# The products of w_ada with c on PE in four column groups, and the recurrent branch's gate projection as four steps

## The chip, the cores and the metric

The kernel runs on one core of a Trainium2 chip. The metric is the device time of one execution in microseconds. PE is the matmul engine (TensorE), PEld its weight loads, DVE the vector engine, ACT the scalar engine, POOL the engine called GpSimd, SP the engine that issues most of the DMAs. One DMA queue of SP carries the weights.

## The reference

All data are float32. There are 256 positions and 1024 channels. A vector c modulates both halves of the block by 6 x 1024 numbers (shift, scale and gate, twice). The part that matters, cut from the reference:

```python
ada = (jax.nn.silu(c) @ w_ada[layer] + b_ada[layer])[:, None, :]
sh1, sc1, g1, sh2, sc2, g2 = jnp.split(ada, 6, axis=-1)
h = rmsnorm(x, norm_pre_mix[layer]) * (1.0 + sc1) + sh1
proj = h @ w_in[layer] + b_in[layer]
xr, gr, q, k, v, gate_r, gate_a = jnp.split(proj, split_points, axis=-1)
xr = causal_depthwise_conv(xr, conv_w[layer], conv_b[layer])
y_rnn = rg_lru(xr, ...) * jax.nn.gelu(gr)
y_att = swa_sink_attention(q.reshape(...), k.reshape(...), v.reshape(...), attn_sinks[layer])
merged = (jax.nn.sigmoid(gate_r) * (y_rnn @ w_o_rnn[layer])
          + jax.nn.sigmoid(gate_a) * (y_att @ w_o_attn[layer]))
mix = merged @ w_out[layer]
x = x + g1 * rmsnorm(mix, norm_post_mix[layer])
h = rmsnorm(x, norm_pre_ffn[layer]) * (1.0 + sc2) + sh2
ff = moe_ffn(h, ...)            # top 4 of 32 experts, each 1024 -> 2 x 1024 -> 1024
x = x + g2 * rmsnorm(ff, norm_post_ffn[layer])
```

w_ada is 1024 x 6144, 24 MiB; xr and gr are 1024 columns of w_in each, 4 MiB each. h can't be formed before sh1 and sc1, that is, before the first third of w_ada has been multiplied with c. The experts' weights are 384 MiB.

## The kernel before

All weights come through a ring of 18 SBUF tiles of 1 MiB (RING), requested by SP in an order written out by hand. The order of work on every engine is that of the code.

**First stage.** x is normalised and transposed (xnT). Then a loop over the 8 blocks k of 128 channels: w_ada's tile for the block holds two outputs' rows (sh1 and sc1 of the block, transposed by the host, so that one output stands in one partition), and `ada_dot` (L130) multiplies each, 128x1024, with silu(c) broadcast over all partitions, and adds up along the row, on DVE. From the two sums come am (L219 and the line behind it) and hT, the block's modulated input (L225). Each weight tile is split (L166, L169) into hi (fp32r, by ACT) and lo = w − hi (half of it by DVE, half by POOL); hT likewise (`split_h`, L184). A product in full precision is then three fp32r products: hi·hTh, hi·hTl, lo·hTh, called terms here. Each k multiplies w_g1, the weights of xr and gr together, 16 groups of 128 outputs, into all 8 PSUM banks (3 with the tag "p", 5 with the tag "a"): 48 products (L235), for k = 0 sixteen in plain f32 (L228).

**Steps.** 26 steps follow, one weight tile of 1 MiB and 256 output channels each, 48 products (`mm_pair`, L259; step 5 `mm_v`, L178): 0 to 4 k and q, 5 v, 6 to 13 the two merge gates, 14 to 17 and 18 to 21 the two output projections, 22 to 25 w_out. A step splits the next step's tile and evacuates the bank of the step before. PLAN says which small tasks stand in the middle of a step's products and which behind them: the recurrence (block-diagonal products L333), the attention (scores L405, transposes L463, values L475) and, as "A", two `ada_dot`s for one of the 16 tiles of w_ada that remain. ISSUE says at which of three points of each step SP requests what: w the next step's weights, a a tile of w_ada, e the first expert's w1.

**Experts.** After w_out (L598 and around) and the router (L714), 32 experts run through the ring (products L963, L996).

Of the kernel before, what the change touches and what calls it, by code (L numbers as in the profile page):

```python
# [32 lines left out]
PLAN = {0: ('', 'g0 s1'), 1: ('', 'h0 c1 s0 c0'), 2: ('A', 'g1 m1 A'), 3: ('R1 A M00 m0', 'h1 A R0 X00'), 4: ('d1 M01', 's3 X01'), 5: ('d0 M02', 'X02 E00 D0 A M10 A'), 6: ('', 'M11 N00 X10 M12'), 7: ('E01 s2 X11 N01', 'X12 T000 A'), 8: ('P00 T010', 'E10 c2 A T011'), 9: ('P01 m2', 'N10 c3 E11'), 10: ('', 'N11 D1 g3 q0 q1 S0 T100'), 11: ('P10 A T110', 'R2 T111 g2 m3'), 12: ('R3 P11', 'h2 A'), 13: ('S1', 'h3 d2 D2 d3 D3 A'), 14: ('', 'q2 S2 q3 y0 S3'), 15: ('A y2', ''), 16: ('y1', 'A'), 17: ('', 'A y3'), 19: ('', 'A A')}  # L33
ISSUE = {-1: 'wwaww', 0: 'aw', 2: 'w', 5: 'a', 8: 'aw', 11: 'w', 14: 'aa', 19: 'aw', 21: 'w', 22: 'aw', 28: 'w', 29: 'w', 31: 'w', 33: 'a', 36: 'aa', 37: 'aw', 42: 'w', 43: 'wawwa', 49: 'w', 50: 'w', 52: 'awa', 54: 'w', 60: 'w', 64: 'e', 69: 'ww', 71: 'e', 72: 'e', 74: 'e', 76: 'eee'}
# [15 lines left out]
def tile_hybrid_block(ctx: ExitStack, tc: tile.TileContext, x_in, c, vecs, rows, w_ada, w_g1, w_qk, w_v, w_gate,  # L50
# [16 lines left out]
    def rtile(shape, name):  # L67
        return ring.tile([P] + list(shape), F32, name=name, tag="w")
# [70 lines left out]
    ada_dot(wada[0], 0, 0)  # L139
# [11 lines left out]
    ada_dot(wada[0], 1, 8)  # L151
# [8 lines left out]
    def split(w, pool=True, mid=lambda: None):  # L160

        hi, lo = [ring.tile([P, 2 * D], F32R, name=n_, tag="w") for n_ in ("hi", "lo")]
        parts = []
        for h in range(2):
            c_ = slice(h * D, (h + 1) * D)
            nc.scalar.activation(hi[:, c_], w[:, c_], AF.Copy)  # L166
            if h == 0:
                mid()
            (nc.gpsimd if h and pool else nc.vector).tensor_tensor(lo[:, c_], w[:, c_], hi[:, c_], op=OP.subtract)  # L169
            parts.append((hi[:, c_], lo[:, c_]))  # L170
        return parts
# [31 lines left out]
    g1b = [bank("p") for _ in range(3)] + [bank("a") for _ in range(5)]  # L203
    PLAIN = 1

    def g1(f):
        return g1b[f // 2][:, (f % 2) * S:(f % 2 + 1) * S]

    for k in range(KC):
        if k:  # L210
            wada.append(rtile((2, D), "w"))
            for n in range(2):
                nc.sync.dma_start(out=wada[k][:, n], in_=w_ada[k, :, n])
            ada_dot(wada[k], 0, k)
            ada_dot(wada[k], 1, 8 + k)
        wt = rtile((2048,), "w")
        for h in range(2):
            nc.sync.dma_start(out=wt[:, h * D:(h + 1) * D], in_=w_g1[k, :, h * D:(h + 1) * D])
        nc.vector.scalar_tensor_tensor(am[:, 0, k:k + 1], ada[:, 8 + k:9 + k], scb[:, k:k + 1], v("n_pre_mix", k),  # L219
                                       op0=OP.add, op1=OP.mult)  # L220
        nc.vector.tensor_tensor(am[:, 1, k:k + 1], ada[:, k:k + 1], vec[:, o_ + k:o_ + k + 1], op=OP.add)
        if k == 1:
            lru_scales()
        hT[k] = t2((S,), name="hT")
        nc.vector.tensor_scalar(hT[k], xnT[:, k], am[:, 0, k:k + 1], am[:, 1, k:k + 1], op0=OP.mult, op1=OP.add)  # L225
        if k < PLAIN:
# [3 lines left out]
        else:  # L230
            whl = split(wt, mid=lambda: split_h(k))
            for h in range(2):
                for i, (m, n) in enumerate(THREE):
                    for f in range(8):
                        nc.tensor.matmul(g1(8 * h + f), whl[h][m][:, f * P:(f + 1) * P], (hTh, hTl)[n][:, k], start=False,  # L235
                                         stop=k == KC - 1 and i == 2, skip_group_check=True)
        if 4 <= k < 4 + PLAIN:
            split_h(k - 4)
# [246 lines left out]
    W = [w_qk[i] for i in range(5)] + [w_v] + [w_gate[i] for i in range(8)]  # L485
# [86 lines left out]

    evac = [ev_k] + [lambda b, i=i: ev_q(i, b) for i in range(4)] + [ev_v]
    evac += [lambda b, i=i: ev_gate(i, b) for i in range(8)]
    evac += [lambda b, i=i: merge_a(i, b) for i in range(4)] + [lambda b, i=i: merge_r(i, b) for i in range(4)]
    for i in range(22):
        if i == 14:
# [3 lines left out]
        if i == 0:  # L581
            for f in range(8):
                b_ = g1b[4 + f // 2][:, (f % 2) * S:(f % 2 + 1) * S]
                nc.vector.tensor_scalar(gr[:, f], b_, v("b_gr", f), None, op0=OP.add)
        run(after)
    nc.vector.tensor_tensor(ada[:, 16:48], ada[:, 16:48], vec[:, o_ + 16:o_ + 48], op=OP.add)
# [750 lines left out]
```

## Time and profile before

| | |
|---|---|
| median of 3 runs | 1278.45 us (1278.22 to 1279.37) |
| the profiled execution | 1279.63 us, its span 1278.0 us |
| busy in the span | PE 1157.3, DVE 525.8, ACT 261.6, POOL 136.9 us |
| first stage (all products of xr and gr) | 14.26 to 72.13 us |
| steps 0 to 21 | 72.13 to about 267 us |
| w_out, router | about 267 to 313 us |
| experts | about 313 us to the end |

Busy times add up the instructions of one engine. The span is the time from the first instruction to the last; the rows further down are stretches, groups and single instructions of the same execution.

### The profile page before, as it was taken

What the parts mean: (1) busy time and instruction counts of PE and PEld (TensorE: products, weight loads), DVE (VectorE), ACT (ScalarE), POOL (GpSimd) and SP (SyncE); (2) the same over time, 40 slices, a digit from 0 to 9 for tenths busy, and PEclk for the clock granted to TensorE, in tenths of its full rate; (3) what the DMA queues carried; (4) which work ended last, traced back from release to release, by engine and by line L of the source; (5) the groups of instructions that cost most, each with busy time, mean ns of one, the idle gap of its engine ahead of it and who ended that gap; (6) DMA issues with size and microseconds to landing.
All of it is one profiled execution on the core that took longest, in us unless ns stands there. A gap on an engine that the chain in (4) does not pass through costs nothing. (4 is left out here: it accounts for less than half of the span.)

```text
span 1278.0 us, 15323 instructions
## 1 busy us (share of the span) xinstructions
PE 1157.3 (91%) x5883; PEld 554.6 (43%) x5883; DVE 525.8 (41%) x914; ACT 261.6 (20%) x482; POOL 136.9 (11%) x79
## 2 busy tenths in 40 slices
PE   7897978879899999999999988988999999999986
PEld 5896768767333333333333222323333333333322
DVE  6999988965332223232223222222033232322222
ACT  4265656324210001100011001100010011100002
POOL 2355555320100000000000000000000000000000
PEclk9998989889989999999999999999999999999998
DMA  9963436667989999999999999999999999999993
GB/s 366 393 240 144 176 119 255 263 262 288 391 329 379 421 421 421 421 422 421 421 420 421 422 422 421 421 421 421 420 421 418 421 422 421 421 420 420 421 420 123
DMA packets 68177, 468.73 MB, mean 367 GB/s; under 512 B 7616, under 2 KB 8000, under 8 KB 13696
## 3 DMA queue, kind: packets, MB, share of 16 engines
q1 hardware_dynamic: 67392, 466.67, 89.1%
q10 hardware_dynamic: 704, 1.01, 0.3%
q8 instruction: 47, 0.77, 0.2%
q14 instruction: 34, 0.28, 0.1%
HBM read 466.61 MB, written 1.05 MB: 366 GB/s over the span
## 5 line engine op out<-in xcount | busy, mean ns | idle before, releaser
L963 PE MATMUL bank_a<-w,xg 128*64 128x512 f32 x2048 | 469.2, 601 | 9.1 <-DMA w<-in_w_dram 8.9
L963 PEld LDWEIGHTS bank_a<-w,xg 128*64 128x64 f32 x2048 | 137.3, 137 | 290.7 <-issue 251.4
L996 PE MATMUL bank_a<-w,aT 128*64 128x512 f32 x960 | 219.6, 602 | 12.9 <-ACT aT L990 7.4
L1044 DVE TENSOR_SCALAR G<-bank_p,slot 128x256 fp32r<-128x256 f32 x32 | 15.5, 484 | 415.6 <-PE bank_p L1039 415.6
L996 PEld LDWEIGHTS bank_a<-w,aT 128*64 128x64 f32 x960 | 65.3, 138 | 150.1 <-issue 108.6
L990 ACT ACTIVATE aT<-bank_p 128x512 f32<-128x512 f32 x31 | 18.5, 597 | 530.6 <-PE bank_p L986 530.6
L1017 DVE TENSOR_TENSOR ff<-ff,bank_p 128x512 f32<-128x512 f32 x124 | 79.6, 683 | 63.5 <-PE bank_p L1014 63.5
L169 POOL TENSOR_TENSOR lo<-w,hi 128x1024 fp32r<-128x1024 f32 x32 | 89.8, 2809 | 132.5 <-ACT hi L166 105.7
L1251 POOL TENSOR_TENSOR os<-os,x 128x512 f32<-128x512 f32 x1 | 1.8, 1821 | 875.4 <-ACT os L1250 875.4
L130 DVE SCALAR_TENSOR_TENSOR w<-w,cs 128x1024 f32<-128x1024 f32 x48 | 89.4, 1900 | 1.1 <-DMA w<-in_w_ada_dram 1.1
L1004 DVE SCALAR_TENSOR_TENSOR ys<-bank_a,gslot,ys 128x512 fp32r<-128x512 f32 x31 | 23.2, 750 | 151.6 <-ACT ys L1003 151.6
L166 ACT ACTIVATE hi<-w 128x1024 fp32r<-128x1024 f32 x66 | 66.1, 1050 | 11.7 <-DVE lo L169 6.8
L1014 PE MATMUL bank_p<-ys,G 64*128 64x512 f32 x248 | 47.3, 457 | 14.1 <-DVE ys L1004 13.5
L1003 ACT ACTIVATE ys<-bank_a,gslot 128x512 fp32r<-128x512 f32 x31 | 21.3, 688 | 172.0 <-PE bank_a L996 168.5
L169 DVE TENSOR_TENSOR lo<-w,hi 128x1024 fp32r<-128x1024 f32 x34 | 49.0, 1445 | 6.9 <-ACT hi L166 6.9
L777 PE MATMUL bank_p<-pm,hth 128*128 128x256 f32 x112 | 33.4, 327 | 13.4 <-DVE pm L759 13.4
L1014 PEld LDWEIGHTS bank_p<-ys,G 64*128 64x128 f32 x248 | 19.3, 191 | 47.0 <-issue 25.2
L777 PEld LDWEIGHTS bank_p<-pm,hth 128*128 128x128 f32 x112 | 22.7, 203 | 35.9 <-issue 18.3
L959 PE MATMUL bank_a<-b1r,pick 128*128 128x512 f32 x124 | 37.7, 423 | 0.0
L976 ACT ACTIVATE ys<-gl 128x512 f32<-128x512 f32 x33 | 20.8, 630 | 69.4 <-DVE gl L975 69.4
L959 PEld LDWEIGHTS bank_a<-b1r,pick 128*128 128x128 f32 x124 | 20.7, 188 | 29.4 <-issue 26.8
L259 PE MATMUL bank_p<-hTh,hi 128*128 128x256 f32 x208 | 31.2, 294 | 0.0
(337 smaller groups left out, 1252.2 us busy)
## 6 DMA issues: line engine op xcount, KB each, us to landing
w<-in_w_dram SPq DMA_DIRECT2D x383, 1024.0 KB, 19.8
w<-in_w_ada_dram SPq DMA_DIRECT2D x16, 1024.0 KB, 5.0
w<-in_w_ada_dram SPq DMA_DIRECT2D x16, 512.0 KB, 10.2
w<-in_w_g_dram SPq DMA_DIRECT2D x16, 512.0 KB, 10.2
w<-in_w_gate_dram SPq DMA_DIRECT2D x8, 1024.0 KB, 5.7
w<-in_w_qk_dram SPq DMA_DIRECT2D x5, 1024.0 KB, 8.1
w<-in_w_oa_dram SPq DMA_DIRECT2D x4, 1024.0 KB, 5.8
w<-in_w_or_dram SPq DMA_DIRECT2D x4, 1024.0 KB, 5.9
```

The costliest lines, as they stand in the source:

```text
L130: nc.vector.scalar_tensor_tensor(wt[:, n], wt[:, n], 1.0, sc_, op0=OP.mult, op1=OP.mult, accum_out=ada[:, j:j + 1])
L166: nc.scalar.activation(hi[:, c_], w[:, c_], AF.Copy)
L169: (nc.gpsimd if h and pool else nc.vector).tensor_tensor(lo[:, c_], w[:, c_], hi[:, c_], op=OP.subtract)
L259: nc.tensor.matmul(b[:, n], w[n][m][:, k * P:(k + 1) * P], z[l][:, k], start=k == 0 and i == 0 and (n == 0 or not late), stop=k == KC - 1 ...
L777: nc.tensor.matmul(ps[:, n], z[:, t, f * P:(f + 1) * P], pms[:, t].rearrange("p a b -> p (a b)"), start=t == 0 and n == 0 if len(ts) == 1 ...
L959: nc.tensor.matmul(o, m.rearrange("p a b -> p (a b)"), z, start=False, stop=False)
L963: nc.tensor.matmul(o[q * CAP:(q + 1) * CAP], xk(k), w1t[k][:, c0:c0 + 512], start=k == 0, stop=k == KC - 1)
L996: nc.tensor.matmul(y[q * CAP:(q + 1) * CAP], aT[:, k % 4, k // 4 * CAP:(k // 4 + 1) * CAP], w2t[k // 2][:, k % 2, q * 512:(q + 1) * 512], ...
L1003: nc.scalar.activation(hi, y, AF.Copy, scale=G[1])
L1004: nc.vector.scalar_tensor_tensor(lo, y, G[1], hi, op0=OP.mult, op1=OP.subtract)
L1014: nc.tensor.matmul(b[q], G[0][qs, t * P:(t + 1) * P], ys[i][qs], start=i == 1, stop=i == 0)
L1017: nc.vector.tensor_tensor(d, d, b[q], op=OP.add)
```

## The change

c comes in as 8 more columns of the small tile of vectors instead of a broadcast of 512 KB. w_ada's tiles hold the same numbers in another order: inputs in partitions, eight blocks of 128 inputs, and for each 256 outputs. `ada_mm` (L136) multiplies each block with a column of silu(c), repeated 32 times as the stationary operand; block k goes to the column group k % 4 of PE, and so to 32 of the bank's 128 partitions, and each group adds up two blocks. ACT copies the bank to SBUF (L140), and `ada_sum` (L147) adds the four groups' rows by a product with a vector (one_each) that has a single 1 in each group, which also brings the outputs back into partitions; DVE copies the two columns out (L148).

The first stage forms xr alone, 24 products for each k (L260; 8 plain ones for k = 0, L248), into four "a" banks, with ada_mm and ada_sum of the next block between the terms. gr becomes steps 6 to 9, evacuated by DVE (`ev_gr`); the steps behind move by four, 30 in all. A task "A" now sums up the tile of the "A" before and multiplies the next. ISSUE requests a step's weights at the start of the step four before it.

```diff
-    def ada_dot(wt, n, j):
-        nc.vector.scalar_tensor_tensor(wt[:, n], wt[:, n], 1.0, sc_, op0=OP.mult, op1=OP.mult,
-                                       accum_out=ada[:, j:j + 1])
+    def ada_mm(wt):
+
+        b = bank("p")
+        for k in range(KC):
+            q = k % 4
+            nc.tensor.matmul(b[32 * q:32 * q + 32, 0:2 * P], sc_[:, k:k + 1].to_broadcast([P, 32]), wt[:, k], start=k < 4,
+                             stop=k >= 4)
+        rows_done[0] += 1
+        r = aux[:, 1, rows_done[0] % 4 * 2 * P:(rows_done[0] % 4 + 1) * 2 * P]
+        nc.scalar.activation(r, b[:, 0:2 * P], AF.Copy)
+        return b, r
+
+    def ada_sum(br, js):
+
+        b, r = br
+        for n in range(2):
+            nc.tensor.matmul(b[:, 2 * P + n:2 * P + n + 1], r[:, n * P:(n + 1) * P], one_each, start=True, stop=True)
+        nc.vector.tensor_copy(ada[:, js[0]:js[1] + 1:js[1] - js[0]], b[:, 2 * P:2 * P + 2])
...
-    g1b = [bank("p") for _ in range(3)] + [bank("a") for _ in range(5)]
+    xrb = [bank("a") for _ in range(4)]
...
+    ada_sum(ada_mm(wada[0]), (0, 8))
+    make_h(0)
+    xw = [None] * 3
+    for k in range(KC):
+        h = k % 2
+        if h == 0:
+            xw = [ring.tile([P, 2 * D], t_, name=n_, tag="w") for n_, t_ in (("w", F32), ("hi", F32R), ("lo", F32R))]
+        wt = xw[0][:, h * D:(h + 1) * D]
+        nc.sync.dma_start(out=wt, in_=w_xr[k])
+        if k >= PLAIN:
+            whl = split_half(*xw, h, False)
...
+        for i, (m, n) in enumerate(THREE):
+            if i == 1 and k + 1 < KC:
+                br = ada_mm(wada[k + 1])
+            if i == 2 and k + 1 < KC:
+                ada_sum(br, (k + 1, 8 + k + 1))
+                make_h(k + 1)
+                if k + 1 >= PLAIN:
+                    split_h(k + 1)
+            if k >= PLAIN:
+                for f in range(KC):
+                    nc.tensor.matmul(xr_of(f), whl[m][:, f * P:(f + 1) * P], (hTh, hTl)[n][:, k], start=False,
+                                     stop=k == KC - 1 and i == 2, skip_group_check=True)
...
     def ada_run(j):
-        for n in range(2):
-            ada_dot(late[j], n, 2 * j + n)
+        ada_sums()
+        sums_due.append((ada_mm(late[j]), (2 * j, 2 * j + 1)))
...
-    W = [w_qk[i] for i in range(5)] + [w_v] + [w_gate[i] for i in range(8)]
+    W = [w_qk[i] for i in range(5)] + [w_v] + [w_gr[i] for i in range(4)] + [w_gate[i] for i in range(8)]
...
+    def ev_gr(i, b):
+        for n in range(2):
+            nc.vector.tensor_scalar(gr[:, 2 * i + n], b[:, n], v("b_gr", 2 * i + n), None, op0=OP.add)
```

On PE, one k of the first stage before (bank_p and bank_a are PSUM banks; hTh and hTl the parts of hT, hi and lo those of the weights):

```order
L235 MATMUL bank_p<-hTh,hi 128x256 x6
L235 MATMUL bank_a<-hTh,hi 128x256 x2
L235 MATMUL bank_p<-hTl,hi 128x256 x6
L235 MATMUL bank_a<-hTl,hi 128x256 x2
L235 MATMUL bank_p<-hTh,lo 128x256 x6
L235 MATMUL bank_a<-hTh,lo 128x256 x2
L235 MATMUL bank_a<-hTh,hi 128x256 x8
L235 MATMUL bank_a<-hTl,hi 128x256 x8
L235 MATMUL bank_a<-hTh,lo 128x256 x8
```

And one k of the first stage of the changed kernel, on PE (sc is silu(c), aux the rows that ACT copied out):

```order
L260 MATMUL bank_a<-hTh,hi 128x256 x8
L136 MATMUL bank_p<-w,sc 32x256 x8
L260 MATMUL bank_a<-hTl,hi 128x256 x8
L147 MATMUL bank_p<-one_each,aux 128x1 x2
L260 MATMUL bank_a<-hTh,lo 128x256 x8
```

Half the products are gone from a k, and the next k's ada_mm and ada_sum stand between its terms.

On ACT, two k of the first stage before (a tile's number is behind its name):

```order
L166 ACTIVATE hi_291<-w_284 128x1024
L184 ACTIVATE hTh_161<-hT_289 128x256
L166 ACTIVATE hi_291<-w_284 128x1024
L166 ACTIVATE hi_359<-w_352 128x1024
L184 ACTIVATE hTh_161<-hT_357 128x256
L166 ACTIVATE hi_359<-w_352 128x1024
```

And two k of the changed kernel, on ACT:

```order
L140 ACTIVATE aux_122<-bank_p_249 128x256
L197 ACTIVATE hTh_161<-hT_272 128x256
L182 ACTIVATE hi_285<-w_284 128x1024
L140 ACTIVATE aux_122<-bank_p_301 128x256
L197 ACTIVATE hTh_161<-hT_324 128x256
L182 ACTIVATE hi_285<-w_284 128x1024
```

Before, the first half of hi stood ahead of hTh; now the one hi of a k stands behind it, and the copy of the w_ada bank ahead of both.

On PE, steps 2 and 3 before (xc is the recurrence's input, cs the tile in which its weights lie, kT and qT are keys and queries):

```order
L259 MATMUL bank_p<-hTh,hi 128x256 x8
L259 MATMUL bank_p<-hTl,hi 128x256 x8
L259 MATMUL bank_p<-hTh,lo 128x256 x8
L333 MATMUL bank_a<-xc,cs 64x256 x8
L259 MATMUL bank_p<-hTh,hi 128x256 x8
L259 MATMUL bank_p<-hTl,hi 128x256 x8
L259 MATMUL bank_p<-hTh,lo 128x256 x8
L405 MATMUL bank_a<-kT,qT 128x128 x8
L333 MATMUL bank_a<-xc,cs 64x256 x8
```

And the same place of the changed kernel, on PE:

```order
L136 MATMUL bank_p<-w,sc 32x256 x8
L284 MATMUL bank_p<-hTh,hi 128x256 x8
L284 MATMUL bank_p<-hTl,hi 128x256 x8
L284 MATMUL bank_p<-hTh,lo 128x256 x8
L364 MATMUL bank_a<-xc,aux 64x256 x8
L147 MATMUL bank_p<-one_each,aux 128x1 x2
L136 MATMUL bank_p<-w,sc 32x256 x8
L284 MATMUL bank_p<-hTh,hi 128x256 x8
L284 MATMUL bank_p<-hTl,hi 128x256 x8
L284 MATMUL bank_p<-hTh,lo 128x256 x8
L147 MATMUL bank_p<-one_each,aux 128x1 x2
L136 MATMUL bank_p<-w,sc 32x256 x8
```

Each "A" is now ten products on PE, the sum of the last tile and the products of the next, where it was two operations on DVE.

## Rows read from the trace of the kernel before

**Rows 1.** Windows: stretch, length; busy PE, PEld, DVE, ACT, POOL; PE clock, DMA share, GB/s.

```profile
14.00:72.00 58.00, 48.94 (x367) 46.54 (x368) 52.53 (x85) 23.35 (x38) 21.68 (x8) 1.00 1.00 397
72.00:267.00 195.00, 168.84 (x1260) 152.35 (x1259) 182.66 (x241) 106.81 (x207) 98.35 (x47) 0.92 0.50 191
267.00:313.00 46.00, 35.82 (x163) 27.29 (x161) 23.67 (x51) 18.50 (x38) 6.45 (x8) 0.85 0.80 311
400.00:1250.00 850.00, 796.04 (x3655) 283.69 (x3652) 224.33 (x413) 82.88 (x148) 0.00 (x0) 0.99 1.01 421
29.38:36.69 7.31, 6.01 (x48) 5.80 (x49) 6.76 (x10) 2.32 (x4) 2.82 (x1) 1.00 1.03 407
218.00:224.00 6.00, 5.57 (x36) 5.58 (x37) 5.78 (x9) 0.75 (x3) 2.44 (x1) 0.72 0.01 3
```

**Rows 2.** Waits in 400:600 (SP) and 600:1000 (PE): total us, times, longest.

```profile
SPq L64 <- PE bank_a L963: 39.9, 29, 4.0
...
PE bank_a L963 <- DMA w<-in_w_dram: 8.9, 19, 0.6
```

**Rows 3.** Timeline, PE, at 284 us: start, length, [idle before it <-releaser].

```profile
283.82 1.11 PE L598 MATMUL bank_p<-ident,ada 128*128 128x128 f32 x4 [8.70 <-DVE t L568]
```

**Rows 4.** Timeline, PE: steps 0 and 3, and the router's products.

```profile
72.13 1.12 PE L259 MATMUL bank_p<-hTh,hi 128*128 128x256 f32 x8
73.09 1.12 PE L259 MATMUL bank_p<-hTl,hi 128*128 128x256 f32 x8
...
89.50 1.94 PE L333 MATMUL bank_a<-xc,cs 64*64 64x256 f32 x16
91.38 1.01 PEld L259 LDWEIGHTS bank_p<-hTh,hi 128*128 128x128 f32 x8 [0.39 <-issue]
...
309.07 1.89 PE L714 MATMUL bank_p<-rw,h2T 128*128 128x32 f32 x16
```

**Rows 5.** Groups by shape, PE, 72:267: busy, mean ns | idle before.

```profile
L475 PE MATMUL bank_a<-t,vv 128*64 128x512 f32 x24 | 9.1, 650 | 7.7 <-DVE t L468 7.7
L333 PE MATMUL bank_a<-xc,cs 64*64 64x256 f32 x64 | 7.8, 382 | 0.0
L463 PE MATMUL bank_a<-ident,att 128*128 128x128 f32 x48 | 7.4, 299 | 0.6 <-POOL att L451 0.6
L405 PE MATMUL bank_a<-kT,qT 64*128 64x256 f32 x32 | 7.3, 490 | 6.5 <-DVE att L424 6.5
L405 PE MATMUL bank_a<-kT,qT 64*128 64x128 f32 x32 | 2.3, 285 | 0.0
```

**Rows 6.** Groups, DVE, 72:267: the dots.

```profile
L130 DVE SCALAR_TENSOR_TENSOR w<-w,cs 128x1024 f32<-128x1024 f32 x32 | 59.3, 1896 | 0.0
```

**Rows 7.** Timeline, 14:37 us: k = 0, and one later k.

```profile
14.25 1.56 ACT L146 ACTIVATE xnT<-bank_a 128x512 f32<-128x512 f32 x3
14.26 2.86 PE L228 MATMUL bank_p<-hT,w 128*128 128x256 f32 x12 [0.85 <-DVE hT L225]
16.95 4.48 PE L228 MATMUL bank_a<-hT,w 128*128 128x256 f32 x20
21.98 0.97 PE L235 MATMUL bank_p<-hTh,hi 128*128 128x256 f32 x6 [0.55 <-ACT hTh L184]
...
28.07 0.22 DVE L219 SCALAR_TENSOR_TENSOR am<-ada,scb,vec 128x1 f32<-128x1 f32 x1
28.91 0.42 ACT L184 ACTIVATE hTh<-hT 128x256 fp32r<-128x256 f32 x1 [4.92 <-DVE hT L225]
29.23 1.99 ACT L166 ACTIVATE hi<-w 128x1024 fp32r<-128x1024 f32 x2
29.38 0.98 PE L235 MATMUL bank_p<-hTh,hi 128*128 128x256 f32 x6 [1.39 <-ACT hTh L184]
...
36.54 1.05 ACT L166 ACTIVATE hi<-w 128x1024 fp32r<-128x1024 f32 x1
36.69 0.39 PE L235 MATMUL bank_p<-hTh,hi 128*128 128x256 f32 x1 [1.30 <-ACT hTh L184]
```

**Rows 8.** DMA issues: x count, KB each, us to landing.

```profile
cs<-in_c_dram SPq DMA_DIRECT2D x1, 512.0 KB, 4.8
```

More of the change, by code (lines that the diff above doesn't have):

```diff
@@ L49, in tile_hybrid_block @@
 @with_exitstack
-def tile_hybrid_block(ctx: ExitStack, tc: tile.TileContext, x_in, c, vecs, rows, w_ada, w_g1, w_qk, w_v, w_gate,
+def tile_hybrid_block(ctx: ExitStack, tc: tile.TileContext, x_in, vecs, rows, w_ada, w_xr, w_gr, w_qk, w_v, w_gate,
                       w_bd, w_or, w_oa, w_o, w_router, w1, b1, w2, b2, out):
@@ L157, in tile_hybrid_block, with split, split_half @@
     nc.vector.memset(xr[:, :, 0:3], 0.0)
-    def split(w, pool=True, mid=lambda: None):
+    def split(w, pool=True):
         hi, lo = [ring.tile([P, 2 * D], F32R, name=n_, tag="w") for n_ in ("hi", "lo")]
[L163 to L171, printed above, removed]
+        return [split_half(w, hi, lo, h, pool) for h in range(2)]
+    def split_half(w, hi, lo, h, pool):
+        c_ = slice(h * D, (h + 1) * D)
+        nc.scalar.activation(hi[:, c_], w[:, c_], AF.Copy)
+        (nc.gpsimd if h and pool else nc.vector).tensor_tensor(lo[:, c_], w[:, c_], hi[:, c_], op=OP.subtract)
+        return hi[:, c_], lo[:, c_]
     THREE = ((0, 0), (0, 1), (1, 0))
@@ L222, in tile_hybrid_block @@
         if k == 1:
             lru_scales()
-        hT[k] = t2((S,), name="hT")
-        nc.vector.tensor_scalar(hT[k], xnT[:, k], am[:, 0, k:k + 1], am[:, 1, k:k + 1], op0=OP.mult, op1=OP.add)
         if k < PLAIN:
-            for f in range(16):
-                nc.tensor.matmul(g1(f), wt[:, f * P:(f + 1) * P], hT[k], start=k == 0 and f % 2 == 0, stop=False,
+            for f in range(KC):
+                nc.tensor.matmul(xr_of(f), wt[:, f * P:(f + 1) * P], hT[k], start=k == 0 and f % 2 == 0, stop=False,
@@ L229, in tile_hybrid_block @@
                                  skip_group_check=True)
[L230 to L236, printed above, removed]
+        for i, (m, n) in enumerate(THREE):
[7 more added lines that the diff above has]
+            if k >= PLAIN:
+                for f in range(KC):
+                    nc.tensor.matmul(xr_of(f), whl[m][:, f * P:(f + 1) * P], (hTh, hTl)[n][:, k], start=False,
+                                     stop=k == KC - 1 and i == 2, skip_group_check=True)
@@ L296, in tile_hybrid_block, with ada_sums @@
     late = {}
+    sums_due = []
+    def ada_sums():
+        while sums_due:
+            ada_sum(*sums_due.pop())
     def ada_run(j):
-        for n in range(2):
-            ada_dot(late[j], n, 2 * j + n)
+        ada_sums()
+        sums_due.append((ada_mm(late[j]), (2 * j, 2 * j + 1)))
     xcs, U = {}, {}
@@ L580, in tile_hybrid_block @@
         step(i, evac[i], lambda: run(mid))
[L581 to L584, printed above, removed]
         run(after)
+    ada_sums()
     nc.vector.tensor_tensor(ada[:, 16:48], ada[:, 16:48], vec[:, o_ + 16:o_ + 48], op=OP.add)
```

92 lines of the change are left out of this document (46 added, 46 removed).

## The prediction

> **What bounds the kernel now.** I read the windows first, one line for each stretch [rows 1]. From 400 us on the experts' weights arrive at 421 GB/s with the DMA engines full (share 1.01). Of the waits behind that, SP waits for PE to free a ring slot early in the stretch (39.9 us on L963 between 400 and 600), and PE waits for weights later (8.9 us between 600 and 1000) [rows 2]. So the stream is as long as its bytes, and it cannot start sooner than the ring (18 tiles of 1 MiB) has room, which PE makes by beginning the experts, at about 313 us. The change touches nothing there. A microsecond gained or lost before 313 us I count as one at the end.
>
> Ahead of it are three stretches [rows 1]. In the first stage (14 to 72 us) one k takes 7.31 us, of which DVE is busy 6.76 and PE 6.01: DVE sets the pace. In the first 22 steps (72 to 267 us) DVE is busy 182.66 us of 195.0, PE 168.84, at a mean clock of 0.92: DVE is nearly full, PE waits 26.2 us, and some windows fall to a granted 0.72, part of the time at 1.2 GHz in place of 2.4. From 267 to 313 us (w_out, router) no line changes. There PE has a wait of 8.70 us, the longest of that stretch, and neither the dots nor gr are in it [rows 3]; I leave it in place, with ±5 us for how the start of that stretch falls.
>
> **What a step of PE costs.** A term of 8 products starts 0.96 us after the one before it, 0.12 us for each product [rows 4]. A step has 48, 5.76 us; 22 steps are 126.7 us. The other PE work of the stretch is 33.9 us in five groups [rows 5]. 168.84 − 126.7 − 33.9 leaves 8.2 us for the slow clock and changes of shape. So PE could get back at most 26.2 + 8.2 = 34 us there.
>
> **gr becomes four steps.** 4 × 5.76 = **+23.0 us** of PE in the steps. In the first stage the same products lay beside DVE's dots and set nothing, so the cover is gone and the price is full. Their evacuations (8 DVE operations of 128x256) fit into what DVE is relieved of. Their 4 MiB of weights leave the first stage's requests on SP for the steps', where the DMA share is 0.50 [rows 1]: nothing on either side of the sum.
>
> **The dots go to PE.** DVE loses 59.3 us of dots in the steps [rows 6]: from 94% busy of 195.0 us to well under 70% of a longer stretch. PE gains, sixteen times in the steps, an ada_mm and an ada_sum. A plain f32 product of 128x256 is two instructions in the trace, each 4.48/20 = 0.224 us [rows 7]. The 8 products of ada_mm, 16 instructions, would take 3.58 us one after another, and 0.9 if all four column groups run at once. The trace shows two tiles side by side but never four: the sixteen instructions of L333 (64x256, on a 64x64 tile) take 91.38 − 89.50 = 1.88 us, where pairs would be 1.79 and one by one 3.58, and at the change of shape behind them the weight loads lose 0.39 us to "issue" [rows 4]. Bounds: 0.85 (four at once, the change hidden), 3.6 to 3.9 (no overlap); two at once with the change is 2.0 to 2.1. I take 1.25: 0.9 and one change of shape, 0.35. An ada_sum is 4 short instructions at 1.89/16 = 0.118 [rows 4], 0.47 us. Sixteen times 1.72 is **+27.4 us** (21 to 40 between four and two at once; 65 if not at all).
>
> On the change of shape the row says up to 0.39 us. The Trainium skill, page "TensorEngine Tiling (Array Packing)", section Key Properties, states that changing the tiling mode drains TensorE, which speaks against this change; the idle 0.39 us agrees. The skill's page "TensorE: Matmul & The Clock Gate", Part 3 (Packing small matmuls), measured three column tiles at 2.38 times, not 3; 3.58/2.38 would be an estimated 1.5 us in place of 0.9, and the sum some 10 us higher. No run here shows it yet.
>
> **What DVE's relief gives back.** PE's largest waits are for DVE (7.7 us at L475, 6.5 at L405) [rows 5], where DVE works off dots queued ahead of the attention's or the recurrence's operations. Without dots I expect most of it, and most of the slow clock, to go: **−26 us** of the 34. Some 8 us stay or come anew: an ada_sum's bank is held until DVE's copy, one of only three "p" banks; behind that copy in line on PE stand the next step's products; ada_sum needs ACT's copy, queued behind splits of 1.05 us. Bounds −17 (half stays) and −34.
>
> **The first stage.** k's products now wait for a longer chain. I add it up from PE's side, beginning at a first product: term 0, 0.96; ada_mm(k+1), 1.25; term 1, 0.96, under which ACT copies the bank (0.42, as hTh's copy of the same size); ada_sum, 0.47 with 0.2 of latency; DVE's copy, 0.15 (am, no larger, took 0.22 with its latency); from am's start to the start of hTh's copy 28.91 − 28.07 = 0.84; that copy, 0.32 (29.23 − 28.91); then ACT's hi, which the order now puts behind hTh, 1.05; and 0.05 [rows 7]. The sum is 6.25 us for one k against 7.31, and PE has 2.88 + 1.72 = 4.6 of work in it: it idles 1.65. DMA needs (1.05 + 0.52) MB at 407 GB/s = 3.9 us, and isn't the bound. Start: xnT is complete at 14.25 + 1.56 = 15.81 [rows 7]; without the 512 KB for c [rows 8], 0.52/397 = 1.3 us sooner, 14.5. ACT's copy of the first bank (0.4), the sum (0.5), DVE's copy (0.15) and 0.84 put k = 0 at 16.5 (before 14.26). Its products are now 8 plain ones, 16 × 0.224 = 3.6; then ada_mm 1.25, ACT 0.5, the sum with latency 0.7, 0.15, 0.84, 0.32 and 1.1 of hi: k = 1 starts at 25.0 (before 21.98). Six periods, 37.5, some 0.7 for the scales on DVE, and the last k's 2.9 end at 66.1, before 72.13 [rows 4]: **−6 us**. DVE is no bound: of its 6.76 us both dots go, and its lo is now for half as many weights. Bounds −12 (hi hidden after all, period 5.2) and −1 (period near 7); with the chain hidden too PE's 4.6 would set it, about −16.
>
> **Sum.** The profiled execution took 1279.63 us (span 1278.0 and 1.6 around it), 1.18 above the median of 1278.45. −6 + 23.0 + 27.4 − 26 = +18.4: 1298.0 for such an execution, **1297 us** as a median.
>
> **Rivals.** (a) The column groups do not run four at once. Two at once: ada_mm about 2.05, +0.8 in 16 places and in 7 periods, +18, 1315. None: +2.5 in 16 and 7 places, +58, about 1355. For it: no row shows four. Against: L333 shows two clearly.
> (b) Faster: PE never waits. DVE was the only bound, and PE then runs without a gap from the first product to the end of the steps. Its work would be 3.6 + 7 × 2.88 + 23 × 1.72 + 26 × 5.76 + 33.9 = 247.1 us, against 267 − 14.26 = 252.7 before, and starts 2.2 later: −3.4, **1275**; with ada_mm at 0.85, −12.6, 1266. For it: DVE's 94%. Against: the chain in the first stage, which leaves 1.65 us idle seven times by my sum. It decides once PE's waits over both stretches stay under some 3.4 us in all (12.6 with the cheap ada_mm).
> (c) No measurable change: what goes onto PE (50.4) is just balanced, by a first stage at its lower bound (−12), all waits and slow clock gone (−34) and an ada_mm of 0.98 us (−4.4): about 1278. It needs three bounds at once.
> (d) The gap goes elsewhere: the same forecast with only half of the waits recovered (−17), 1306. That lies inside my likeliest case.
>
> **How the numbers follow.** A measurement of this kernel tells about 0.2% (2.5 us) from no change. My forecast with its own spread, 1283 to 1312, has 0.57; rival (a) 0.17, of which 0.05 for none at once; (b) 0.18; (c) 0.08. Faster is (b), 0.18; same (c), 0.08; slower the rest, 0.74. The range 1273 to 1318 takes in the forecast, two groups at once, (c) and the milder half of (b); it leaves out the cheap end of (b) and serial column groups.
>
> **What would show it.** In the trace after: L136's sixteen instructions within about 1.25 us each time (0.9 to 1.0 busy); the first stage with starts of a k 6.25 us apart and PE waiting for ACT's hi about 1.6 us; its end near 66; the last step before w_out ending near 285 and the first expert near 331; DVE under 70% busy in the steps; PE's waits there under 10 us and its clock near 1.00; from 400 us on nothing but a shift. It would be wrong if the experts' stretch shortened or lengthened by itself; if PE's waits for DVE stayed (another operation, not the dots, set them); if ada_mm's banks, "p" being only three, made steps wait for ACT and DVE; or if the plainer order of weight requests left a step waiting for a tile, which the steps' DMA share of 0.50 makes unlikely [rows 1].

## The result and the profile after

The changed kernel takes **1296.15 us** (median of 4 runs, 1292.51 to 1296.57) where the kernel before took 1278.91 in the same runs: ratio 1.0126, interval 1.0105 to 1.0148. Slower, 0.85 us from the 1297 predicted. But the terms are not those of the prediction. Four points in each trace show it: the first product of step 0, the first product of w_out (L178, after: L191), the first product of an expert (L963, after: L998), and the end of the span. (In the kernel before the first product of an expert starts at 322.95 us; the 313 us named ahead is ten too early.) Times further down are medians without two slow executions, one of e7_hybrid (1383.85 us) and one of e12_late (1961.3 us).

| kernel | first stage ends | steps last | w_out and router last | experts last | span |
|---|---|---|---|---|---|
| before | 72.1 | 194.7 | 56.1 | 955.0 | 1278.0 |
| after | 71.6 | 224.3 | 45.4 | 953.5 | 1294.9 |
| difference | −0.5 | +29.6 | −10.7 | −1.5 | +16.9 |
| predicted | −6 | +24.4 | 0 | 0 | +18.4 |

The windows of the changed kernel, columns as in [rows 1]: two k of the first stage, the steps, a piece of them, w_out with the router, and a stretch of the experts.

```profile
26.39:34.12 7.73, 6.29 (x45) 4.60 (x45) 5.13 (x24) 1.75 (x3) 0.00 (x0) 0.78 1.03 401
34.12:40.31 6.19, 4.75 (x45) 3.83 (x45) 2.51 (x7) 1.75 (x3) 0.00 (x0) 1.00 1.01 394
71.62:295.94 224.32, 207.92 (x1770) 186.47 (x1769) 133.70 (x198) 124.82 (x238) 105.07 (x54) 0.95 0.53 200
208.00:216.00 8.00, 0.41 (x2) 0.41 (x3) 7.75 (x8) 7.24 (x13) 4.79 (x3) 0.70 0.51 190
295.90:341.40 45.50, 42.80 (x224) 33.95 (x223) 25.48 (x70) 20.98 (x41) 5.03 (x4) 1.00 0.75 284
418.00:1268.00 850.00, 796.78 (x3650) 284.03 (x3647) 223.03 (x409) 82.28 (x148) 0.00 (x0) 0.99 1.01 420
```

In the steps DVE fell from 182.66 to 133.70 us busy, and PE's idle time from 26.2 to 16.4 only (224.32 − 207.92). The last line repeats the experts' line of [rows 1]: they are only shifted.

One k of the first stage, after (start, length, engine, line; in brackets the idle time before):

```profile
34.12 1.21 PE L260 MATMUL bank_a<-hTh,hi 128*128 128x256 f32 x8 [1.43 <-ACT hi L182]
35.26 1.07 PE L136 MATMUL bank_p<-w,sc 128*32 128x256 f32 x16
36.26 1.01 PEld L260 LDWEIGHTS bank_a<-hTl,hi 128*128 128x128 f32 x8 [0.41 <-issue]
36.40 0.39 ACT L140 ACTIVATE aux<-bank_p 128x256 f32<-128x256 f32 x1 [2.33 <-PE bank_p L136]
37.31 0.50 PE L147 MATMUL bank_p<-one_each,aux 128*128 128x1 f32 x4
37.92 0.16 DVE L148 COPY ada<-bank_p 128x2 f32<-128x2 f32 x1 [2.60 <-PE bank_p L147]
38.89 0.42 ACT L197 ACTIVATE hTh<-hT 128x256 fp32r<-128x256 f32 x1 [2.11 <-DVE hT L227]
39.22 1.04 ACT L182 ACTIVATE hi<-w 128x1024 fp32r<-128x1024 f32 x1
40.31 1.96 PE L260 MATMUL bank_a<-hTh,hi 128*128 128x256 f32 x8 [1.44 <-ACT hi L182]
42.20 1.87 PE L136 MATMUL bank_p<-w,sc 128*32 128x256 f32 x16
```

From 35.26 to 36.26 sixteen instructions of L136 are through in 1.00 us; four column groups at once would take 0.9, two 1.79. The chain is the one that was added up, hi at its end, and the period 6.19 us against 6.25 (single links are off by up to 0.25 us and cancel). The next k starts at half speed: its term takes 1.96, its L136 1.87. Three of the six periods are of that kind (7.73, 7.92, 7.73 us).

All waits of PE in the steps (total us, times, longest), and the longest where it stands:

```profile
PE bank_p L284 <- DVE ada L148: 8.2, 1, 8.2
PE bank_a L494 <- POOL att L482: 5.7, 1, 5.7
PE bank_p L147 <- ACT aux L140: 2.4, 2, 1.9
```

```profile
204.74 4.36 DVE L411 TENSOR_TENSOR_SCAN rnn<-rnn 128x256 f32<-128x256 f32 x2
205.90 0.50 PE L147 MATMUL bank_p<-one_each,aux 128*128 128x1 f32 x4
206.33 1.07 PE L136 MATMUL bank_p<-w,sc 128*32 128x256 f32 x16
...
211.43 0.69 DVE L399 SCALAR_TENSOR_TENSOR rnn<-t,rnn 128x512 f32<-128x512 f32 x1
212.30 2.62 POOL L183 TENSOR_TENSOR lo<-w,hi 128x1024 fp32r<-128x1024 f32 x1 [2.13 <-issue]
212.82 2.65 DVE L399 SCALAR_TENSOR_TENSOR rnn<-t,rnn 128x512 f32<-128x512 f32 x1
215.39 0.15 DVE L148 COPY ada<-bank_p 128x2 f32<-128x2 f32 x1
215.59 2.08 PE L284 MATMUL bank_p<-hTh,hi 128*128 128x256 f32 x8 [8.19 <-DVE ada L148]
```

The sum was ready at 206.4, its copy of 0.15 us ran at 215.39, behind the recurrence on DVE, and the bank that it held was the next step's. The recurrence was itself slow there: the same operation, L399, took 0.69 us alone and 2.65 with POOL's half of a weight split beside it (2.62 us). No run takes that half away from POOL.

### The profile page after: what moved, and what is told of

Its sections match the earlier page's. It is cut to its first block, busy times and chain, and to the rows that moved or that the text cites. A ratio compares the mean times of both kernels' runs of the same rounds, so it can differ in the third digit from the quotient of the medians.

```text
span 1294.9 us, 16295 instructions
## 1 busy us (share of the span) xinstructions
PE 1188.7 (92%) x6371; PEld 574.0 (44%) x6371; DVE 441.6 (34%) x851; ACT 272.5 (21%) x506; POOL 121.6 (9%) x76
## 3 DMA queue, kind: packets, MB, share of 16 engines
HBM read 466.08 MB, written 1.05 MB: 361 GB/s over the span
## 5 line engine op out<-in xcount | busy, mean ns | idle before, releaser
L998 PE MATMUL bank_a<-w,xg 128*64 128x512 f32 x2048 | 470.6, 603 | 8.2 <-DMA w<-in_w_dram 8.2
L998 PEld LDWEIGHTS bank_a<-w,xg 128*64 128x64 f32 x2048 | 137.9, 138 | 290.6 <-issue 254.9
L183 POOL TENSOR_TENSOR lo<-w,hi 128x1024 fp32r<-128x1024 f32 x29 | 76.8, 2654 | 162.7 <-ACT hi L182 136.5
L182 ACT ACTIVATE hi<-w 128x1024 fp32r<-128x1024 f32 x67 | 66.8, 1048 | 3.9 <-POOL lo L183 3.8
L183 DVE TENSOR_TENSOR lo<-w,hi 128x1024 fp32r<-128x1024 f32 x38 | 52.6, 1387 | 30.9 <-ACT hi L182 29.9
L1049 PE MATMUL bank_p<-ys,G 64*128 64x512 f32 x248 | 47.6, 460 | 14.1 <-DVE ys L1039 13.5
L284 PE MATMUL bank_p<-hTh,hi 128*128 128x256 f32 x272 | 42.5, 302 | 8.2 <-DVE ada L148 8.2
L284 PEld LDWEIGHTS bank_p<-hTh,hi 128*128 128x128 f32 x272 | 37.2, 203 | 14.7 <-DVE ada L148 9.6
L284 PE MATMUL bank_p<-hTl,hi 128*128 128x256 f32 x272 | 40.5, 294 | 0.0
L284 PE MATMUL bank_p<-hTh,lo 128*128 128x256 f32 x272 | 39.1, 287 | 0.0
```

Of the source, the lines that this page charges most:

```text
L284: nc.tensor.matmul(b[:, n], w[n][m][:, k * P:(k + 1) * P], z[l][:, k], start=k == 0 and i == 0 and (n == 0 or not late), stop=k == KC - 1 ...
L998: nc.tensor.matmul(o[q * CAP:(q + 1) * CAP], xk(k), w1t[k][:, c0:c0 + 512], start=k == 0, stop=k == KC - 1)
L1049: nc.tensor.matmul(b[q], G[0][qs, t * P:(t + 1) * P], ys[i][qs], start=i == 1, stop=i == 0)
```

## The experiments

The theory after the result: (1) four groups run at once and are what makes the dots bearable on PE; (2) gr's steps and the tasks cost their full time on PE, and DVE's relief gave back less than they cost; (3) hi on the chain and PE's idle time, which slows its clock, cost the first stage its gain; (4) the stall before the first expert [rows 3] has to do with requests and went by chance. The rival to each stands in the expectations. The measured columns of all kernels together, the last four from the profiled execution of each. Intervals that overlap that of the changed kernel (1.0105 to 1.0148), as those of e3, e5 and e11 do, show no difference from it in time; there only the stretches of the traces speak.

| run | time | ratio to before, interval | first stage | steps | w_out, router | experts |
|---|---|---|---|---|---|---|
| e1_wide | 1343.26 | 1.0502, 1.0472 to 1.0533 | 84.0 | 254.1 | 46.5 | 953.5 |
| e2_hi | 1288.53 | 1.0072, 1.0050 to 1.0094 | 61.8 | 224.0 | 47.0 | 955.7 |
| e3_ahead | 1292.77 | 1.0110, 1.0071 to 1.0150 | 71.8 | 219.5 | 46.4 | 954.2 |
| e4_noada | 1273.48 | 0.9945, 0.9928 to 0.9961 | 71.6 | 197.3 | 47.6 | 955.4 |
| e5_tail | 1302.16 | 1.0163, 1.0132 to 1.0194 | 71.3 | 224.1 | 54.0 | 954.9 |
| e6_before_tail | 1278.69 | 1.0001, 0.9990 to 1.0013 | 71.9 | 195.4 | 54.6 | 956.8 |
| e7_hybrid | 1286.76 | 1.0050, 1.0033 to 1.0067 | 73.2 | 202.3 | 53.2 | 956.2 |
| e8_hi_ahead | 1284.20 | 1.0042, 1.0028 to 1.0056 | 61.8 | 219.4 | 46.3 | 953.8 |
| e9_before_b1 | 1273.16 | 0.9955, 0.9942 to 0.9969 | 72.1 | 195.4 | 47.7 | 956.3 |
| e10_best | 1275.67 | 0.9981, 0.9970 to 0.9993 | 73.0 | 201.1 | 46.0 | 954.3 |
| e11_busy | 1294.63 | 1.0125, 1.0106 to 1.0143 | 66.8 | 223.9 | 47.0 | 955.1 |
| e12_late | 1279.62 | 1.0007, 0.9995 to 1.0018 | 73.4 | 204.1 | 46.0 | 953.5 |

**e1_wide: no column groups.**

```diff
-            q = k % 4
-            nc.tensor.matmul(b[32 * q:32 * q + 32, 0:2 * P], sc_[:, k:k + 1].to_broadcast([P, 32]), wt[:, k], start=k < 4,
-                             stop=k >= 4)
+            nc.tensor.matmul(b[:, 0:2 * P], sc_[:, k:k + 1].to_broadcast([P, P]), wt[:, k], start=k == 0,
+                             stop=k == KC - 1)
```

> The changed kernel with the w_ada products at full width: silu(c) repeated 128 times as the stationary operand, eight products one after another into the whole bank, no column groups; the sum takes one of the 128 equal rows. Theory (the four groups run at once, 1.00 us for the sixteen instructions of L136, and at this price they are what makes the step bearable): 3.58 us each, +2.5 us in 16 places of the steps and in 7 periods of the first stage, less some of the 18 us of waits and slow clock: 1335 to 1355 us. Rival (the changes of the tile's shape cost what the groups save, or waits swallow it): within 10 us of 1296.

```profile
107.19 3.70 PE L134 MATMUL bank_p<-w,sc 128*128 128x256 f32 x16
113.60 0.50 PE L145 MATMUL bank_p<-ident,aux 128*128 128x1 f32 x4
113.99 3.72 PE L134 MATMUL bank_p<-w,sc 128*128 128x256 f32 x16
```

The timeline of PE in the steps: 3.7 us in place of 1.00. 1343.26 us, 47 more than the changed kernel; the steps take 29.8 us more, not 16 × 2.7 = 43: PE's work there grows by 36.7 us and its idle time falls by 7.0 (16.4 to 9.4). The rival falls: the groups, with their changes of the tile's shape, are worth 47 us.

**e2_hi: hi of the next k ahead, in the first stage.** The next k's split is called before this k's products, so that ACT has hi done before hTh.

```diff
+    nxt = get_x(0)
+    for k in range(KC):
...
-        if k >= PLAIN:
-            whl = split_half(*xw, h, False)
+        wt, whl = nxt
         if k + 1 < KC:
...
+            nxt = get_x(k + 1)
```

> The changed kernel, where in the first stage ACT's hi of the next k (and DVE's lo) stands ahead of the copy of the w_ada bank, not behind hTh; the DMAs are in the same order. Theory (the 1.05 us of hi is on the chain from one k to the next, and PE's idle 1.43 us there is what lets its clock fall): the period falls from 7.04 us on average to about 5.2, the granted clock stays at 1.00, and the steps begin 5 to 11 us sooner: 1285 to 1291 us. Rival 1 (the weights' DMA sets the first stage): period and time unchanged. Rival 2 (the clock falls for another reason): the period falls by 1 us, the slow periods stay: 1290 us. Rival 3 (what is gained ahead of the steps is lost in them, because DVE or ACT set them): start of the steps sooner, time within 2 us of 1296.

```profile
32.20 1.21 PE L265 MATMUL bank_a<-hTh,hi 128*128 128x256 f32 x8 [0.49 <-ACT hTh L197]
33.34 1.07 PE L136 MATMUL bank_p<-w,sc 128*32 128x256 f32 x16
...
37.45 1.21 PE L265 MATMUL bank_a<-hTh,hi 128*128 128x256 f32 x8 [0.49 <-ACT hTh L197]
```

PE's timeline: the period is 5.25 us (once 5.68), PE waits 0.49 for hTh (once 0.92), and behind the first of the six periods the half speed is gone. The steps begin 9.8 us sooner, the time is 7.6 us shorter. Rivals 1 and 2 fall, rival 3 in the main: 1.6 us of the gain are lost between w_out and the first expert and about 2 behind it.

**e11_busy: PE kept busy in the first stage's gap**, hi where it was; the ten products have no reader.

```diff
+    spare = bank("a")
...
+        if PLAIN <= k < KC - 1:
+            for f in range(10):
+                nc.tensor.matmul(spare[:, 0:S], whl[0][:, 0:P], hTh[:, k], start=True, stop=True)
```

> The changed kernel with ten idle products of 0.12 us into a spare bank behind each k of the first stage from k = 1, where PE waits 1.43 us for hi. Theory (PE's idle time is what lets its clock fall in that stage, four of six periods at 7.7 us and two at 6.2): all periods 6.2 to 6.4, granted clock 1.00, the steps begin 4 to 5 us sooner, 1291 to 1293 us. Rival (the slow periods have another cause, DVE's or the weights'): same periods, 1296 us or a little more.

(Three of six periods were slow in the changed kernel, not four.) The windows of two k, columns as above, and the products of k = 0 in the changed kernel and here:

```profile
24.62:32.34 7.72, 7.48 (x54) 5.99 (x54) 5.13 (x24) 1.75 (x3) 0.00 (x0) 0.78 1.03 408
32.34:38.55 6.21, 5.97 (x55) 5.05 (x55) 2.52 (x7) 1.75 (x3) 0.00 (x0) 1.00 1.03 404
```

```profile
16.39 5.41 PE L248 MATMUL bank_a<-hT,w 128*128 128x256 f32 x16 [1.09 <-DVE hT L227]
16.30 3.72 PE L249 MATMUL bank_a<-hT,w 128*128 128x256 f32 x16 [1.10 <-DVE hT L228]
```

From the second period on all are 6.2 to 6.5 us with no work taken away; the first, behind a gap of 2.49 us, is still slow. The six periods take 39.2 us in place of 42.3. These 3.1 us are the filler's, so the slow periods that it reached came from PE's idle time. The steps begin 4.8 us sooner, but 1.7 of that lie in k = 0, ahead of any added product, and are not the edit's. The first stage ends at 66.8 us; the prediction said 66.1. In the time next to nothing of it shows: 1294.63 us is above the range expected, and the ratio to before is that of the changed kernel (1.0125 against 1.0126).

**e3_ahead: the task A of step 13 ahead of S1.**

```diff
-13: ('S1', 'h2 h3 d2 D2 d3 D3 A')
+13: ('A S1', 'h2 h3 d2 D2 d3 D3')
```

> The changed kernel with the task A of step 13 moved from behind h2, h3, d2, D2, d3, D3 to the middle of the step, ahead of S1. Theory (PE's wait of 8.2 us for DVE's copy at 208 us is the bank of the sum, held while the copy stands behind the recurrence's operations on DVE): that wait goes, and with it some 3 us of half clock behind it: 1285 to 1289 us. Rival (DVE is full in this stretch, 7.8 us of 8, and the wait comes back at the next step's lo): 1292 to 1297 us.

```profile
PE bank_a L494 <- POOL att L482: 5.7, 1, 5.7
PE bank_p L147 <- ACT aux L140: 2.4, 2, 1.9
PE bank_p L136 <- ACT mgate L318: 2.4, 1, 2.4
PE bank_p L284 <- DVE rnn L408: 0.9, 1, 0.9
```

The waits of PE in the steps: the 8.2 us are gone, 3.8 came anew, 2.9 of them for ACT's evacuations of the gates (L318, 2.4 above and another 0.5) and 0.9 for DVE. The steps are 4.8 us shorter; the time is 3.4 us shorter, which lies within the spread and in the rival's range. Both theories were half right. **e8_hi_ahead**, both edits together:

> Both edits of the changed kernel together: hi ahead in the first stage, and the task A of step 13 ahead of S1. Theory: the two gains lie in different stretches and add up, some 14 to 20 us: 1276 to 1282 us, level with the kernel before. Rival (what starts sooner waits at the next place): no better than the better one of the two.

1284.20 us, 12.0 less than the changed kernel (7.6 + 3.4 apart). In the trace both gains stand side by side (first stage 61.8, steps 219.4): they add up. It misses the range expected, 1276 to 1282, and is still slower than before.

**e4_noada: the 16 later tiles are loaded and not multiplied.**

```diff
     def ada_run(j):
-        ada_sums()
-        sums_due.append((ada_mm(late[j]), (2 * j, 2 * j + 1)))
+        pass
```

The modulation behind the first stage is then the bias alone.

> The changed kernel without the products and sums of the 16 later tiles of w_ada (their tiles are still loaded; the modulation behind the first stage is the bias alone). Theory (a task A is 1.43 us of PE, and the waits for the copies at L148 and L140 hang on it): 16 x 1.43 = 22.9 us and 10.6 us of waits with part of the slow clock fewer in the steps, 1260 to 1265 us. Rival 1 (PE's work of the tasks lies where PE would wait for DVE or POOL anyway): 1275 to 1285 us. Rival 2 (my price before the run, 1.72 each and no waits): 1268 us.

```profile
PE bank_p L285 <- DVE rnn L408: 3.8, 1, 3.8
PE bank_p L285 <- DVE lo L184: 3.4, 1, 3.4
```

The steps are 27.0 us shorter, the time 22.7; 1273.48 us lies in none of the three ranges. PE's work falls by 24.3 us (207.92 to 183.62), 16 × 1.43 = 22.9 and some slow clock; its idle time falls by 2.7 only (16.4 to 13.7), because PE then waits for a lo that stands behind the recurrence on DVE, twice (3.8 and 3.4 us; L408 is the operation behind the first of them). That the 27.0 us come near my price before the run, 16 × 1.72, is two misses that cancel.

**e7_hybrid: the dots of the steps on PE, the first stage and gr as before.**

```diff
     def ada_run(j):
-        for n in range(2):
-            ada_dot(late[j], n, 2 * j + n)
+        ada_sums()
+        sums_due.append((ada_mm(late[j]), (2 * j, 2 * j + 1)))
```

> One half of the change alone: the kernel before with its first stage as it is (dots on DVE, gr under them), and only the 16 later tiles of w_ada on PE in four column groups; 26 steps, PLAN and ISSUE of before. Theory (gr's four steps cost their full 23 us, the 16 tasks cost 22.9 us of PE and give back 16 us of waits and slow clock, and the stall before the first expert is that of before): about 1278 + 22.9 - 16 = 1285 us. Rival 1 (with DVE free PE runs almost without a gap, the 34 us of waits and slow clock go): 1268 to 1275 us. Rival 2 (gr fills gaps of PE in the steps and costs little there): 1296 us or more.

(The cut shows the core of the edit; c, one_each and the later tiles' order come as in the changed kernel.)

```profile
PE bank_p L285 <- DVE ada L153: 4.1, 1, 4.1
PE bank_p L141 <- DVE mg L593: 2.7, 1, 2.7
```

1286.76 us. The steps are 7.6 us longer than before: the tasks cost 22.9, by the length of their instructions, and DVE's relief gave back 15.3. From here to the changed kernel the steps grow by another 22.0 with gr's four (4 × 5.76 = 23.0) and the plan and requests that go with them. Both rivals fall.

**e5_tail and e6_before_tail: the requests of the last steps exchanged.** First the changed kernel with the pattern of before, then the reverse; the entries are cut from ISSUE.

```diff
-66: 'w', 69: 'w', 72: 'w', 75: 'w', 76: 'e', 78: 'e', 81: 'e', 84: 'e', 86: 'e', 87: 'e', 88: 'e'
+66: 'w', 72: 'w', 76: 'e', 81: 'ww', 83: 'e', 84: 'e', 86: 'e', 88: 'eee'
```

> The changed kernel with the requests of its last seven steps in the pattern of the kernel before (the last two tiles of w_out together and late, then the first expert's). Theory (the 10.7 us that the changed kernel gains between the last step and the first expert come from its requests: the kernel before asks for seven expert tiles in one burst at the moment when ACT asks for b1, which then lands 5 us later, twice): PE's wait of about 8.7 us at L633 comes back, 1303 to 1308 us. Rival (the gain comes from elsewhere, from ACT or DVE being less loaded there): within 2 us of 1296.

```diff
-60: 'w', 64: 'e', 69: 'ww', 71: 'e', 72: 'e', 74: 'e', 76: 'eee'
+60: 'w', 63: 'w', 64: 'e', 66: 'we', 69: 'e', 72: 'e', 74: 'e', 75: 'e', 76: 'e'
```

> The kernel before with the requests of its last steps in the plainer pattern of the changed kernel: w_out's last two tiles one step at a time, and the first expert's tiles spread over the last steps. Theory (requests alone make the stall of 8.7 us before the first expert): the stall goes, 1267 to 1271 us. Rival (the stall comes from DVE or ACT being late in the kernel before): 1277 to 1280 us.

ACT's timeline, first in the changed kernel, then twice in e5_tail; and PE's wait in e6_before_tail:

```profile
298.20 1.15 ACT L654 ACTIVATE b1r<-t 128x512 fp32r<-128x512 f32 x2 [6.11 <-DMA t<-in_b_dram]
298.45 0.63 ACT L654 ACTIVATE b1r<-t 128x512 fp32r<-128x512 f32 x1 [6.98 <-DMA t<-in_b_dram]
304.12 0.63 ACT L654 ACTIVATE b1r<-t 128x512 fp32r<-128x512 f32 x1 [5.04 <-DMA t<-in_b_dram]
PE bank_p L598 <- DVE t L568: 8.6, 1, 8.6
```

In the changed kernel ACT waits once for b1, the experts' bias that it converts (L654); the old pattern adds a second wait of 5.04 us, a wait of 4.4 us on PE at L633 (not the 8.7 expected) and 8.6 us to that stretch. The time is 6.0 us longer, just under the range expected and within the spread. In the kernel before the new pattern takes nothing away: PE's wait is 8.6 us where it was 8.7. So requests can make part of the stall, but in the kernel before they aren't enough to undo it.

**e9_before_b1: in the kernel before, b1's conversion behind the first w_out products**, its loads where they were.

```diff
-    for h in range(2):
-        nc.scalar.activation(b1r[:, h], b1t[h], AF.Copy)
-        nc.vector.tensor_tensor(b1r[64:, h], b1t[h][64:], b1r[64:, h], op=OP.subtract)
...
         if i == 22:
+            for h in range(2):
+                nc.scalar.activation(b1r[:, h], b1t[h], AF.Copy)
+                nc.vector.tensor_tensor(b1r[64:, h], b1t[h][64:], b1r[64:, h], op=OP.subtract)
             shifts()
```

> The kernel before with b1's conversion (two copies on ACT, two subtractions on DVE) moved behind the first w_out products, the loads where they were. Theory (the stall before the first expert is ACT, whose next weight split stands in line behind a copy that waits for b1's second half): the wait of 8.7 us at L598 goes, and what starts sooner is kept to the end: 1269 to 1272 us. Rival (the weights behind it are late as well, SP's queue having stood still for 14 us on a buffer of b2's load): the wait moves on, 1276 to 1280 us.

First the kernel before, then e9:

```profile
280.34 0.63 ACT L619 ACTIVATE b1r<-t 128x512 fp32r<-128x512 f32 x1 [5.03 <-DMA t<-in_b_dram]
280.87 1.99 ACT L166 ACTIVATE hi<-w 128x1024 fp32r<-128x1024 f32 x2
281.00 0.69 DVE L620 TENSOR_TENSOR b1r<-t,b1r 64x512 fp32r<-64x512 f32 x1 [4.97 <-ACT b1r L619]
283.09 0.68 DVE L568 SCALAR_TENSOR_TENSOR t<-mgate,bank_p 128x512 f32<-128x512 f32 x1
```

```profile
272.71 2.00 ACT L166 ACTIVATE hi<-w 128x1024 fp32r<-128x1024 f32 x2 [2.81 <-DMA t<-in_b_dram]
278.38 0.62 ACT L808 ACTIVATE b1r<-t 128x512 fp32r<-128x512 f32 x1
281.12 0.63 ACT L808 ACTIVATE b1r<-t 128x512 fp32r<-128x512 f32 x1 [2.12 <-DMA t<-in_b_dram]
```

The hi of the next w_out tile runs at 272.71, where it stood behind b1 until 280.87 before. On DVE the operation that frees PE's bank (L568) stood behind b1's subtraction as well, and both engines' parts were moved, so which of the two held PE isn't separated. PE's wait at L598 is gone, the stretch is 8.4 us shorter, the time 5.3 (expected 1269 to 1272). **1273.16 us, the fastest of the kernels that do the whole work, and nothing of the change is in it.**

**e10_best and e12_late: e7_hybrid with its waits treated one by one**, b1's conversion moved in both; the entries are cut from PLAN.

```diff
-13: ('S1', 'h3 d2 D2 d3 D3 A'), 14: ('', 'q2 S2 q3 y0 S3'), 15: ('A y2', '')
+13: ('A S1', 'h3 d2 D2 d3 D3'), 14: ('', 'q2 S2 q3 y0 S3'), 15: ('y2', 'A')
```

> The kernel before with its first stage, the 16 later tiles of w_ada on PE in four column groups, the task A of step 13 ahead of S1 and that of step 15 behind the step (each stood behind DVE operations that its bank waits for), and b1's conversion moved behind the first w_out products. Theory (three separate waits of PE, 4.1, 2.7 and 7.6 us in the half change alone, go with their causes): 1270 to 1275 us, faster than both kernels. Rival (DVE and ACT set these stretches in any case): 1282 to 1287 us.

1275.67 us, just above the range expected, faster than before by 0.19% (interval 0.07 to 0.30), slower than e9. Two of the three waits went (4.1 to 0.8, and 7.6 to nothing), the third grew from 2.7 to 5.7:

```profile
PE bank_p L141 <- DVE mg L593: 5.7, 1, 5.7
```

e12_late puts that A behind step 18 instead (`15: ('y2', ''), 18: ('', 'A')`).

> As the last of these versions (first stage of before, the 16 later tiles on PE, A of step 13 ahead of S1, b1's conversion later), but the task A of step 15 goes behind step 18, where DVE has finished the recurrence. Theory (PE waited 5.7 us at L141 for a bank that DVE evacuates behind the scans, and ran at half clock for a moment behind it; from step 17 on DVE is free): the wait goes, 1268 to 1271 us, faster than the kernel before with b1's conversion moved alone (1273). Rival (without the A there PE waits at the next product of the steps for the same scans, since yr is made from them): 1273 to 1276 us.

```profile
PE bank_p L285 <- DVE mg L593: 8.1, 1, 8.1
```

1279.62 us, above both ranges, but the rival had the mechanism: with the A away, a product of the steps waits 8.1 us at the same place, for the same evacuation behind the scans. What stands there is the recurrence on DVE; the A had filled part of the gap.

## Why the prediction was right, and where it wasn't

- *The experts are shifted one for one.* Within 2 us of the kernel before in every run (953.5 to 956.8 us).
- *gr's four steps, +23.0.* 22.0 between e7_hybrid and the changed kernel. Right.
- *The dots on PE, +27.4.* L136 takes 1.00 us and a sum 0.43, 16 × 1.43 = 22.9: mis-sized by 4.5, because the change of shape is nearly hidden: 0.41 us of the weight loads' time, and on PE about 0.1 (the term behind it takes 1.05 us where one without a change takes 0.96). The Trainium skill, page "TensorE: Matmul & The Clock Gate", Part 3 (Packing small matmuls), would have given an estimated 1.5 us; here four groups gained 3.6 times (3.58 to 1.00 us). The drain that the Trainium skill's page "TensorEngine Tiling (Array Packing)", section Key Properties, states was a small price here: those 0.41 us.
- *DVE's relief, −26 with bounds −17 and −34.* This is the step that failed, by 9.7 us: the steps grew by 29.6, not by 23.0 + 22.9 = 45.9, so 16.3 came back, just outside the bound. Some 6.5 of it is slow clock and changes of shape, of 8.2; of the 26.2 us of waits 9.8 went where 18 were reckoned. The wait for DVE's copy was named, but "some 8 us" was meant for all of them; that one alone took 8.2, POOL's normalisation of the attention 5.7, ACT's copy 2.4. So PE's waits aren't under 10 us, and one of the prediction's own signs of being wrong is there: "p" banks that make steps wait for ACT and DVE. e3, e10 and e12 show why it can't all be had: where one wait goes, ACT's evacuations (e3) or those behind DVE's scans (e10, e12) make the next one.
- *The first stage, −6.* −0.5. The chain was right to 0.06 us where the clock was granted in full; left out was that the clock falls in this stage (0.78 in a slow period): three of six periods take some 1.5 us more, and k = 0's products 5.41 us where 3.6 were reckoned. e11 shows PE's idle time to be the cause for 3.1 us of it. The rows gave no sign of it: the kernel before stood still nearly as long, 1.30 and 1.39 us in a period of 7.31 [rows 7], at a clock of 1.00 [rows 1]. What makes the difference between 1.3 us in 7.3 and 1.4 in 6.2, no run shows.
- *w_out and router, 0 ± 5.* −10.7. The stall of [rows 3] was taken for a fixture. e9 shows it is the order of work on ACT and DVE (hi and the evacuation behind a copy that waits for b1). The traces show two parts of its loss. ACT asks for b1 3.3 us ahead of w_out's first product in the changed kernel and in e5 (3.5), 2.6 us behind it in the kernel before and in e6 (2.7). And b1's second half comes some 5 us after the first in all of these but the changed kernel. Its copy so starts 13.5 us behind w_out's first product in the kernel before and e6, 8.8 in e5, some 3 in the changed kernel. Why the new requests don't bring the second half sooner in e6 isn't settled.

So the sum is right (+16.9 of 18.4) by luck, because the misses cancel: +5.5 and +5.2 in the first stage and the steps, −10.7 and −1.5 behind them. Rival (a) fell by L136's 1.00 us, (b) by PE's 16.4 us of idle time in the steps, (c) with the result. Rival (d) had the waits right, 16.3 us against its 17; what kept the time from its 1306 is the stall that went.

## What to carry to other kernels

Here, work that was moved from a full engine to one that was nearly full cost its whole time there, and gave back only the waits that no other work on the first engine would have made: dots of 59.3 us on DVE gave back 15 to 16 on PE. Work that lay under another engine's bound, gr under the dots, set nothing where it was and cost nearly all of its time where it went. Before an engine's load is moved, look at the longest single wait of the trace: two copies with their subtractions, moved behind the next products, gained more (5.3 us) than any version with the dots on PE. And when a forecast comes true, compare its terms too.

## What the runs showed of the hardware

Eight f32 products of 128x256 in four column groups of 32 took 1.00 us, the same at full width 3.7. With gaps of 1.43 to 1.74 us on PE in each period three of six ran partly at half speed, the first of them behind a gap of 2.49; with gaps of 0.24 to 0.92 us (e2, e11) none did; the first period of both, behind 1.54 and 2.49 us, was slow as well. Yet gaps of 1.30 and 1.39 us in periods of 7.31 left the clock at 1.00 in the kernel before. One and the same operation of DVE took 0.69 us alone and 2.65 beside an operation of POOL.
